# The first expert's tokens: seven tiles gathered early, the eighth put in by a one-hot matmul, and expert blocks 96 wide

## The chip, the cores and the metric

The kernel runs on one core of a Trainium2 chip. The metric is the device time of one execution in microseconds (us). The engines are PE (TensorE: matmuls and transposes), DVE (VectorE), ACT (ScalarE), POOL (GpSimd) and SP (SyncE, which here only issues DMAs). Each engine works through its own instructions in order; semaphores tie the engines together.

## The reference

One layer on 1024 tokens of width 1024: a norm and a wide projection, dilated attention and an RWKV7 branch, an output projection, and then a mixture of experts, which is where the change lies. A router picks one of four groups and two of its eight experts for each token. Cut to what matters:

```python
x = x + mixed @ w_out
h = rms_norm(x, norm2_gain)
grp_prob = softmax(h @ w_group_router + b_group_router); grp_p, grp_idx = top_k(grp_prob, 1)
sel_logits = (h @ w_expert_router + b_expert_router)[group grp_idx]          # 8 of 32
top_p, top_i = top_k(softmax(sel_logits), 2)
gates = grp_p * top_p / sum(top_p); expert_id = grp_idx * 8 + top_i
# for each expert e, over the tokens that chose it (at most two experts a token):
hid = silu(xb @ w_expert_gate[e]) * (xb @ w_expert_up[e])                    # 1024 -> 512
y[token] += gate * (hid @ w_expert_down[e])                                  # 512 -> 1024
x = x + y
```

All of it is float32.

## The kernel before

Products are made at float32 accuracy from two halves: every operand is split into a rounded `hi` and the rest `lo`, and each product is three matmuls (hi x hi, lo x hi, hi x lo).

**The output projection** runs over eight tiles of 128 tokens (the loop `for i in range(8)`), each in two column halves `c`. Behind its matmuls, a tile is added to the residual (`xt`, DVE), multiplied by the norm's gain to `h2` (POOL, or DVE for the last half) and written to HBM (`dH2`, and `out`). `router(i)` transposes `xt` on PE (four transposes for each half), ACT copies them to `hT`, and PE multiplies by the router's weights. `route(i)` is a long chain of small DVE operations: logits `lg`, the two best experts, their one-hots `roh`, a running count over tokens (matmul `pp`), and from it each token's slot within its expert. A one-hot of the slot (`rslot`) times `roh` is summed over all eight tiles in the PSUM tile `pT`: for slot q and expert e it holds the token's index, gate and norm factor. The pieces of `route` are generator steps that `rstep()` interleaves with the next tile's matmuls; behind the last tile they have nothing beside them.

**The experts.** Each of the 32 experts has 96 slots (`CAP`; what goes beyond is done in a branch behind, which this input does not reach). `tbl` is the table of token indices, read from `pT` with 2^20 added, so that an empty slot lies out of bounds. `gather` fetches an expert's rows of `dH2` by an indirect DMA that POOL issues, into one of two `xin` tiles that were zeroed before. `xpose` turns them: eight PE transposes, ACT copies the rounded half (`xTh`), DVE makes the rest (`xTl`). The block is 128 wide there, with 32 rows of zeros. 48 matmuls of 512 columns give gate and up, ACT (Silu) and DVE make `hd` of them, four more transposes give `hTh` and `hTl`, 24 matmuls do the down projection, DVE and ACT scale the result by the gate into `row`, and `add_rows` adds its 96 rows to `out` by an indirect accumulating DMA. Padding rows go to spare rows behind the output (`tba`).

**The weights** of the experts come as 384 chunks of 512 KB, twelve an expert, in the order in which PE wants them: gate and up of expert 0, of expert 1, down of expert 0, gate and up of expert 2, down of expert 1 and so on. Each chunk is split by ACT (`hi`) and DVE (`lo`) into one of nine `u` pairs. The first eight chunks are loaded straight into four of these pairs, so the splits 5 to 8 must wait until the two raw chunks in their pair have been split; from the ninth on, a split waits until PE has used the pair. All later chunks land in a ring of areas (`areas`, 23 of them); a chunk's area is loaded again when its `lo` has been made.

What sets the order: the program is written with a scheduler that orders instructions by priority, except where `manual_schedule` fixes the order as written for some engines. Here DVE, ACT, SP and POOL are fixed from the last tile on until the first expert's transposes are issued.

Of the kernel before, what the change touches and what calls it, by code (L numbers as in the profile page):

```python
# [10 lines left out]
F32 = mybir.dt.float32  # L11
# [35 lines left out]
NPH = 2  # L47
# [5 lines left out]
NL3 = 1  # L53
# [129 lines left out]
def block_kernel(ctx, tc, I, out, dbg=None):  # L183
# [1037 lines left out]
    def route(i, pl, r2):  # L1221
# [106 lines left out]
    p8s = s9.enter_context(tc.tile_pool(name="p8s", bufs=2, reuse_waits="tile"))  # L1328
    s8b = ExitStack()
# [66 lines left out]
    pT = pb([128])  # L1396
# [11 lines left out]
    def split_next(n):  # L1408
        for _ in range(n):
# [6 lines left out]
            hi, lo = pair[:, 0], pair[:, 1]  # L1416
            nc.scalar.activation(hi, raw, AF.Copy)  # L1417
            nc.vector.tensor_tensor(lo, raw, hi.bitcast(F32), op=ALU.subtract)  # L1418
            chunks[key] = (hi, lo)
            cursor[0] += 1  # L1420
            if i >= N0 and i + NR < len(order):
                load_raw(i + NR)

    tailm = ExitStack()
    for i in range(8):
# [3 lines left out]
        h2 = p8.tile([128, S], F32, name="h2", bufs=BH2)  # L1429
# [3 lines left out]
        for c in range(2):  # L1433
# [13 lines left out]
            if i == 7 and c == 1:  # L1447
# [3 lines left out]
                rstep()  # L1451
                tailm.enter_context(tc.manual_schedule(engines={mybir.EngineType.DVE, mybir.EngineType.Activation,
# [36 lines left out]
    xin = [pm.tile([128, D], F32, name=f"xin{i}") for i in range(2)]  # L1489
    row = pm.tile([128, D], F32, name="row")  # L1490
    for t in xin:
        nc.gpsimd.memset(t, 0.0)
# [10 lines left out]
    def gather(dst, src, idx):  # L1503
        dst = dst[0:idx.shape[0]]
        nc.gpsimd.indirect_dma_start(out=dst, out_offset=None, in_=src,  # L1505
                                     in_offset=bass.IndirectOffsetOnAxis(ap=idx, axis=0),
                                     bounds_check=S - 1, oob_is_err=False)
# [27 lines left out]
    gather(xin[0], dH2, tbl[0:CAP, 0:1])  # L1535
# [14 lines left out]
    tailm.close()  # L1550
    tpad = pm.tile([128, 2], F32, name="tpad")
    nc.vector.tensor_scalar(tpad[:, 0:1], tokid[:, 0:1], float(S), None, op0=ALU.add)
    nc.vector.tensor_scalar(tpad[:, 1:2], tpad[:, 0:1], -1.0, float(1 << 20), op0=ALU.mult, op1=ALU.add)
    tba = pm.tile([128, 32], I32, name="tba")
    tocc = pm.tile([128, 32], F32, name="tocc")
    nc.vector.tensor_scalar(tocc, pT[:, 96:128], tpad[:, 1:2], tpad[:, 0:1], op0=ALU.mult, op1=ALU.add)
    nc.vector.tensor_tensor(tba, tocc, pT[:, 0:32], op=ALU.add)
# [5 lines left out]
    for m, e in steps:  # L1563
        if m == 0:
# [4 lines left out]
            for c in range(4):  # L1569
# [133 lines left out]
```

## Time and profile before

| | |
|---|---|
| median of 3 runs | 1723.49 us (1723.04 to 1726.64) |
| the profiled execution | 1724.65 us, its span 1722.9 us |
| PE busy | 96% of the span |
| output projection's last matmul | begins at 1108.27 us |
| first expert's first matmul | begins at 1127.26 us |
| second expert's first matmul | begins at 1143.01 us |
| last matmul | ends at 1710.47 us |

All times are in us from the span's start. Between the projection's last matmul and the first expert's lies a stretch with little on PE; from about 1143 us on PE is never idle until the last two experts.

### The profile page before, as it was taken

To read this page: it belongs to the slowest core of one execution; us is meant where nothing else is said; L and a number is where in the kernel's file an instruction comes from. 1 tells how busy PE (TensorE), PEld (TensorE's weight loads), DVE (VectorE), ACT (ScalarE), POOL (GpSimd) and SP (SyncE) were. 2 spreads that over 40 slices of the span, in tenths; PEclk is the share of its full clock that TensorE was granted. 3 is DMA by queue.
4 is the path that set the end of the run, shared out by engine and by line. 5 is a ranking of instruction groups with operands and counts; after the bars stand their busy time and mean duration, and the time that the engine had idled before them with its cause. 6 is when DMAs were issued, how large, how long until landed. Compare 5 with 4: busy or idle time off the path is not lost. (4 is left out here: it accounts for less than half of the span.)

```text
span 1722.9 us, 25856 instructions
## 1 busy us (share of the span) xinstructions
PE 1646.6 (96%) x9395; PEld 1307.5 (76%) x9396; DVE 1193.8 (69%) x2181; ACT 870.6 (51%) x1315; POOL 290.7 (17%) x314
## 2 busy tenths in 40 slices
PE   8999998999999999999998899889999999999996
PEld 6677777777777777777776677668888888888884
DVE  5638798784553444444335756689999999998985
ACT  4524444423221333344342122378888888887774
POOL 0101103133430000000100221112221222211211
PEclk9999999999999999999998999989999999999998
DMA  8324324466642111111249774679999999999993
GB/s 296 124 85 132 120 86 154 141 239 196 210 140 69 37 44 45 36 41 53 74 146 268 225 288 147 224 255 378 378 375 364 375 375 373 364 370 365 367 370 110
DMA packets 145619, 363.44 MB, mean 211 GB/s; under 512 B 17316, under 2 KB 62772, under 8 KB 145484
## 3 DMA queue, kind: packets, MB, share of 16 engines
q1 hardware_dynamic: 123108, 303.67, 48.9%
q0 software_dynamic: 15872, 50.35, 10.4%
q10 hardware_dynamic: 6504, 7.69, 1.6%
q8 instruction: 76, 1.25, 0.3%
q14 instruction: 59, 0.48, 0.1%
HBM read 307.49 MB, written 62.29 MB: 215 GB/s over the span
## 5 line engine op out<-in xcount | busy, mean ns | idle before, releaser
L1532 PE MATMUL pb<-u,xTh 128*128 128x512 f32 x1024 | 338.6, 406 | 0.5 <-ACT xTh L1527 0.5
L307 PE MATMUL pa<-xlo,wh 128*128 128x512 f32 x736 | 304.9, 414 | 0.0
L307 PE MATMUL pa<-xhi,wh 128*128 128x512 f32 x736 | 300.2, 408 | 2.9 <-DVE qT L905 1.4
L307 PE MATMUL pa<-xhi,wl 128*128 128x512 f32 x736 | 297.9, 405 | 2.3 <-DVE wl L278 2.3
L1418 DVE TENSOR_TENSOR u<-raw,u 128x1024 fp32r<-128x1024 f32 x216 | 254.8, 1221 | 18.6 <-ACT u L1417 15.9
L1417 ACT ACTIVATE u<-raw 128x1024 fp32r<-128x1024 f32 x216 | 223.6, 1056 | 31.6 <-PE pb L1532 18.4
L1532 PEld LDWEIGHTS pb<-u,xTh 128*128 128x128 f32 x1024 | 191.3, 189 | 40.4 <-ACT xTh L1527 1.3
L1532 PE MATMUL pb<-u,xTl 128*128 128x512 f32 x512 | 207.7, 406 | 0.3 <-DVE xTl L1528 0.3
L307 PEld LDWEIGHTS pa<-xlo,wh 128*128 128x128 f32 x736 | 139.9, 190 | 39.1 <-issue 10.3
L307 PEld LDWEIGHTS pa<-xhi,wh 128*128 128x128 f32 x736 | 139.9, 190 | 36.1 <-issue 2.2
L307 PEld LDWEIGHTS pa<-xhi,wl 128*128 128x128 f32 x736 | 139.9, 190 | 33.4 <-DVE wl L278 3.2
L1418 DVE TENSOR_TENSOR u<-mix,u 128x1024 fp32r<-128x1024 f32 x128 | 151.6, 1221 | 11.2 <-ACT u L1417 9.3
L1532 PE MATMUL pa<-u,hTh 128*128 128x512 f32 x512 | 143.4, 401 | 0.9 <-ACT hTh L1527 0.9
L1417 ACT ACTIVATE u<-mix 128x1024 fp32r<-128x1024 f32 x128 | 133.2, 1057 | 16.6 <-PE pb L1532 9.0
L980 DVE SCALAR_TENSOR_TENSOR Sb<-pb,rqk,bias 128x128 f32<-128x128 f32 (+1 forms) x96 | 35.5, 407 | 124.5 <-PE pb L979 116.6
L1511 POOL DMA_INDIRECT out<-row,tba x30 | 78.8, 2627 | 202.1 <-ACT u L1417 171.5
L1532 PEld LDWEIGHTS pb<-u,xTl 128*128 128x128 f32 x512 | 96.9, 189 | 18.5 <-DVE xTl L1528 1.0
L1532 PEld LDWEIGHTS pa<-u,hTh 128*128 128x128 f32 x512 | 93.5, 188 | 22.4 <-ACT hTh L1527 1.5
L276 ACT ACTIVATE wh<-wr 128x1024 fp32r<-128x1024 f32 x49 | 51.8, 1057 | 112.3 <-PE pa L307 106.2
L1532 PE MATMUL pa<-u,hTl 128*128 128x512 f32 x256 | 80.7, 396 | 1.2 <-DVE hTl L1528 1.2
L1505 POOL DMA_INDIRECT xin<-dH,tbl x32 | 38.5, 1204 | 250.3 <-PE pb L1526 247.5
L984 ACT ACTIVATE Sb<-Sb,ML 128x128 f32<-128x128 f32 (+1 forms) x96 | 42.3, 441 | 54.7 <-DVE ML L982 54.7
(415 smaller groups left out, 2829.5 us busy)
## 6 DMA issues: line engine op xcount, KB each, us to landing
raw<-in_w_expert_up SPq DMA_DIRECT2D x72, 512.0 KB, 11.8
raw<-in_w_expert_gate SPq DMA_DIRECT2D x71, 512.0 KB, 5.4
raw<-in_w_expert_down SPq DMA_DIRECT2D x71, 512.0 KB, 11.7
wr<-in_w_in SPq DMA_DIRECT2D x49, 512.0 KB, 3.6
mix<-in_w_expert_down SPq DMA_DIRECT2D x46, 512.0 KB, 13.2
mix<-in_w_expert_gate SPq DMA_DIRECT2D x42, 512.0 KB, 4.9
mix<-in_w_expert_up SPq DMA_DIRECT2D x40, 512.0 KB, 11.9
dGA<-gs POOLq DMA_DIRECT2D x32, 256.0 KB, 2.9
```

The costliest lines, as they stand in the source:

```text
L276: nc.scalar.activation(wh, wr, AF.Copy)
L307: nc.tensor.matmul(ps, a[:, k, :], b[:, k, hs], start=(n == 0), stop=(n == 23))
L980: nc.vector.scalar_tensor_tensor(Sb[:, hh, 0:nk], pS[:, 0:nk], u.rn[:, 0, i, hh:hh + 1], u.bias[:, hh, 256 - nk:], op0=ALU.mult, op1=ALU.add)
L984: nc.scalar.activation(Sb[:, hh, 0:nk], Sb[:, hh, 0:nk], AF.Exp, bias=u.ML[:, i, hh:hh + 1], accum_out=u.ML[:, i, 2 + hh:3 + hh])
L1417: nc.scalar.activation(hi, raw, AF.Copy)
L1418: nc.vector.tensor_tensor(lo, raw, hi.bitcast(F32), op=ALU.subtract)
L1505: nc.gpsimd.indirect_dma_start(out=dst, out_offset=None, in_=src, in_offset=bass.IndirectOffsetOnAxis(ap=idx, axis=0), bounds_check=S - 1, ...
L1511: nc.gpsimd.indirect_dma_start(out=out, out_offset=bass.IndirectOffsetOnAxis(ap=idx, axis=0), in_=src, in_offset=None, compute_op=ALU.add)
L1532: nc.tensor.matmul(ps, x, w, start=first, stop=last)
```

## The change

**The gather.** After tile 6, the table of the first seven tiles is closed (`t6`, and `tb6` for expert 0), and expert 0's rows of tiles 0 to 6 are gathered at once (`xin0`). Tile 7 gets a table of its own (`pTs[1]`), and the two are added for `tbl`. For tile 7's own tokens, `route` makes a one-hot `sel` (token by slot of expert 0), and PE multiplies tile 7's `h7` by it. Both go into one PSUM pair `pt0`: eight transposes of `xin0` start it, eight one-hot matmuls add to it (`turn0`).

**The order.** Three `hi` splits are now ahead of `xTh` of expert 0 on ACT, the others behind it. PE too is written out by hand until expert 0's `hd`, and expert 1's transposes and evacuations come where they are written.

**The width.** Transposes, their evacuations, the stationary operand of all expert matmuls, `hd` and `row` are 96 wide or use 96 rows. `add_rows` uses `tbl`, so empty slots are out of bounds and not written; `tba` and what made it are gone. `NPH` falls from 2 to 0, so there are 21 areas.

```diff
-NPH = 2
+NPH = 0
-NL3 = 1
+NL3 = 3
...
+        if i == 7:
+            ps_ = p8s.tile([128, 2], F32, name="p0", bufs=1)
+            nc.vector.tensor_tensor(ps_[:, 1:2], oh[:, 0, 3, 0:1], oh[:, 1, 3, 0:1], op=ALU.add)
+            nc.vector.tensor_copy(ps_[:, 0:1], pp[:, 0:1])
+            nc.vector.tensor_scalar(sel, rc[:, 72:72 + CAP], ps_[:, 0:1], ps_[:, 1:2], op0=ALU.is_equal, op1=ALU.mult)
...
-            nc.tensor.matmul(pT, slots[s_], oh[:, s_].rearrange("q a e -> q (a e)"), start=(i == 0 and s_ == 0),
-                             stop=(i == 7 and s_ == 1), skip_group_check=True)
+            nc.tensor.matmul(pTs[i // 7], slots[s_], oh[:, s_].rearrange("q a e -> q (a e)"),
+                             start=(i in (0, 7) and s_ == 0), stop=(i in (6, 7) and s_ == 1), skip_group_check=True)
...
+    def turn0(src, by, first):
+        sv = src.rearrange("q (p k) -> q k p", k=8)
+        for k in range(8):
+            nc.tensor.matmul(pt0[k // 4][:, k % 4], sv[:, k], by, start=(first and k % 4 == 0),
+                             stop=(not first and k % 4 == 3), skip_group_check=True)
...
+        if i == 7:
+            pt0 += [pb([4, CAP]) for _ in range(2)]
+            with tc.high_priority(offset=200):
+                turn0(xin0[0:CAP], ident[0:CAP, 0:CAP], True)
         yield from route(i, pl, r2)
...
+                nc.vector.tensor_scalar(t6[:, 0:32], pTs[0][:, 0:32], float(1 << 20), None, op0=ALU.add)
+                nc.vector.tensor_copy(t6[:, 32:96], pTs[0][:, 32:96])
+                nc.vector.tensor_copy(tb6, t6[:, 0:1])
+                nc.gpsimd.memset(xin0, 0.0)
+                gather(xin0, dH2[0:S - 128], tb6[0:CAP], S - 128)
+                pTs[1] = pb([128])
...
+    pem.enter_context(tc.manual_schedule(engines={mybir.EngineType.PE, mybir.EngineType.DVE,
+                                                  mybir.EngineType.Activation, mybir.EngineType.SP,
+                                                  mybir.EngineType.Pool}))
+    turn0(h7, sel, False)
+    split_hi(NL3)
     rstep()
...
-    nc.vector.tensor_scalar(tbl, pT[:, 0:32], float(1 << 20), None, op0=ALU.add)
-    nc.vector.tensor_copy(gr, pT[:, 32:96])
+    split_lo(1)
+    xTn = [pm.tile([128, 8, CAP], F32R, name="xT" + n) for n in "hl"]
+    for q in range(2):
+        nc.scalar.activation(xTn[0][:, 4 * q:4 * q + 4], pt0[q], AF.Copy)
+    for q in range(2):
+        nc.vector.tensor_tensor(xTn[1][:, 4 * q:4 * q + 4], pt0[q], xTn[0][:, 4 * q:4 * q + 4].bitcast(F32),
+                                op=ALU.subtract)
+    split_lo(1)
+    nc.vector.tensor_tensor(tbl, t6[:, 0:32], pTs[1][:, 0:32], op=ALU.add)
+    nc.vector.tensor_tensor(gr, t6[:, 32:96], pTs[1][:, 32:96], op=ALU.add)
...
-                                     in_=src, in_offset=None, compute_op=ALU.add)
+                                     in_=src, in_offset=None, bounds_check=S - 1, oob_is_err=False, compute_op=ALU.add)
...
-            pt = pb([4, 128])
+            pt = pb([4, CAP])
             for j in range(4):
-                nc.tensor.transpose(pt[:, j], sv[:, 4 * q + j], ident)
+                nc.tensor.transpose(pt[:, j], sv[0:CAP, 4 * q + j], ident[0:CAP, 0:CAP])
...
-        nc.tensor.matmul(ps, x, w, start=first, stop=last)
+        nc.tensor.matmul(ps[0:CAP], x, w, start=first, stop=last)
...
                 if e == 0 and c == 3:
-                    xTn = xpose_hi(xin[1], 8, "xT")
+                    xTn = xpose(xin[1], 8, "xT")
...
-            add_rows(rw, tba[0:CAP, e:e + 1])
+            add_rows(rw, tbl[0:CAP, e:e + 1])
```

What this does to the order on the engines is seen at three places. First PE behind the projection's last matmul, before (L1380 transposes tile 7's `xt`, L1392 is the router, L1277 sums the slots, L1526 transposes expert 0's rows):

```order
L1092 MATMUL pa<-woh_7999,mxl 128x512
L1380 MATMUL pb<-ident,xt 128x128 x4
L1392 MATMUL pb<-wr_8584,hT 128x36 x4
L1259 LDWEIGHTS tri
L1259 MATMUL pb<-rA,tri 128x32
L1260 LDWEIGHTS tri
L1260 MATMUL pb<-Acum,tri 128x32
L1277 MATMUL pb<-roh,rslot 128x128 x2
L1538 LDWEIGHTS tri
L1538 MATMUL pb<-Acum,tri 128x32
L1526 MATMUL pb<-ident,xin_9910 128x128 x8
```

And with the change (L1401, L1413 and L1283 are the same three, L1390 is `turn0`, L1588 expert 0's first matmuls):

```order
L1092 MATMUL pa<-woh_7999,mxl 128x512
L1401 MATMUL pb<-ident,xt 128x128
L1390 MATMUL pb<-ident,xin_8576 128x96 x8
L1401 MATMUL pb<-ident,xt 128x128 x3
L1413 MATMUL pb<-wr_8589,hT 128x36 x4
L1259 LDWEIGHTS tri
L1259 MATMUL pb<-rA,tri 128x32
L1260 LDWEIGHTS tri
L1260 MATMUL pb<-Acum,tri 128x32
L1390 MATMUL pb<-sel,h_8575 128x96 x8
L1283 MATMUL pb<-roh,rslot 128x128 x2
```

The eight transposes of the gathered rows have moved from behind the slot sums to a place among tile 7's own transposes, ahead of the router; the one-hot matmuls are new.

Second, ACT from the last routing operation on, before (L1417 is a `hi` split, L1527 `xTh`, L1585 the Silu of `hd`; the first `xTh` pair is expert 0's, the second expert 1's):

```order
L1417 ACTIVATE u<-u 128x1024 x7
L1527 ACTIVATE xTh<-pb 128x512 x2
L1417 ACTIVATE u<-raw_8601 128x1024
L1417 ACTIVATE u<-raw_8603 128x1024
L1417 ACTIVATE u<-raw_8605 128x1024
L1417 ACTIVATE u<-raw_8607 128x1024
L1417 ACTIVATE u<-raw_8609 128x1024
L1417 ACTIVATE u<-raw 128x1024 x2
L1585 ACT_TABLE_LOAD
L1585 ACTIVATE hd<-pb,gr 128x512
L1527 ACTIVATE xTh<-pb 128x512 x2
```

And with the change (L1443 is the `hi` split, L1555 and L1583 are `xTh`):

```order
L1443 ACTIVATE u<-u 128x1024 x3
L1555 ACTIVATE xTh<-pb 128x384 x2
L1328 DMA mxh<-in_w_expert_up 128x1024
L1330 DMA mxh<-in_w_expert_down 128x1024
L1443 ACTIVATE u<-u 128x1024 x5
L1443 ACTIVATE u<-raw_8606 128x1024
L1443 ACTIVATE u<-raw_8608 128x1024
L1443 ACTIVATE u<-raw_8610 128x1024
L1443 ACTIVATE u<-raw_8612 128x1024
L1443 ACTIVATE u<-raw_8614 128x1024
L1443 ACTIVATE u<-raw 128x1024 x3
L1583 ACTIVATE xTh<-pb 128x384 x2
```

Expert 0's `xTh` comes after three splits where it came after eight. Expert 1's comes after sixteen, as against fifteen splits, the table load and `hd` before.

Third, PE at the turn from expert 0 to expert 1 with the change (before, the eight transposes stood singly among expert 0's last twenty matmuls):

```order
L1588 MATMUL pb<-u,xTh 96x512 x2
L1588 MATMUL pb<-u,xTl 96x512
L1582 MATMUL pb<-ident,xin_9936 128x96 x8
L1588 MATMUL pb<-u,xTh 96x512 x4
L1588 MATMUL pb<-u,xTl 96x512
```

Expert 1's transposes have moved behind all of expert 0's matmuls, and four of expert 1's matmuls stand ahead of its first one that needs `xTl`.

## Rows read from the trace of the kernel before

**Rows 1.** Busy time, share of the span and instructions of PE (the page).

```profile
PE 1646.6 (96%) x9395; PEld 1307.5 (76%) x9396; DVE 1193.8 (69%) x2181; ACT 870.6 (51%) x1315; POOL 290.7 (17%) x314
```

**Rows 2.** Timeline of PE: start, duration, operation; in brackets the idle time before.

```profile
1109.45 0.66 PE L1380 MATMUL pb<-ident,xt 128*128 128x128 f32 x4 [0.78 <-DVE xt L1463]
...
1116.67 1.36 PE L1277 MATMUL pb<-roh,rslot 128*128 128x128 f32 x4 [1.24 <-DVE roh L1276]
...
1125.43 1.94 PE L1526 MATMUL pb<-ident,xin 128*128 128x128 f32 x8 [6.69 <-DMA xin<-dH,tbl]
1127.26 1.22 PE L1532 MATMUL pb<-u,xTh 128*128 128x512 f32 x2
```

**Rows 3.** Timeline of DVE in the same stretch.

```profile
1112.36 0.22 DVE L1226 SCALAR_TENSOR_TENSOR lg<-pb,r,br 128x4 f32<-128x4 f32 x1
...
1118.07 0.19 DVE L1498 TENSOR_SCALAR tbl<-pb 128x32 int32<-128x32 f32 x1 [0.89 <-PE pb L1277]
...
1118.46 1.22 DVE L1418 TENSOR_TENSOR u<-u 128x1024 fp32r<-128x1024 f32 x1
...
1119.86 6.90 DVE L1418 TENSOR_TENSOR u<-u 128x1024 fp32r<-128x1024 f32 x6
```

**Rows 4.** Timeline of ACT in the same stretch, up to the second expert's start.

```profile
1114.69 1.04 ACT L1417 ACTIVATE u<-u 128x1024 fp32r<-128x1024 f32 x1
...
1116.51 3.90 ACT L1417 ACTIVATE u<-u 128x1024 fp32r<-128x1024 f32 x4 [0.78 <-issue]
1121.12 1.06 ACT L1417 ACTIVATE u<-u 128x1024 fp32r<-128x1024 f32 x1 [0.71 <-DVE u L1418]
...
1142.37 1.08 ACT L1527 ACTIVATE xTh<-pb 128x512 fp32r<-128x512 f32 x2
```

**Rows 5.** Timeline of POOL from tile 7's first half on.

```profile
1102.46 1.28 POOL L1467 TENSOR_TENSOR h<-xt,g 128x512 f32<-128x512 f32 x1 [5.74 <-DVE xt L1463]
...
1119.14 1.47 POOL L1505 DMA_INDIRECT xin<-dH,tbl  x1 [2.49 <-issue]
```

**Rows 6.** DMA issues, 1095 to 1150: median us from issue to landing.

```profile
xin<-dH,tbl POOLq DMA_INDIRECT x4, 5.7
```

**Rows 7.** The gathers of 1150 to 1200, by tile: issue to landing.

```profile
DMA to landing us min/median/max: 7.7/7.8/8.2
```

**Rows 8.** Timeline of PE: the second expert's first matmuls.

```profile
1143.01 0.97 PE L1532 MATMUL pb<-u,xTh 128*128 128x512 f32 x3 [0.54 <-ACT xTh L1527]
```

**Rows 9.** Busy time by stretch: length, engines, granted clock (PEclk), DMA share, GB/s.

```profile
903.20:907.80 4.60, 0.01 (x1) 0.00 (x0) 2.21 (x4) 0.63 (x1) 0.00 (x0) 0.99 0.99 364
907.80:911.20 3.40, 3.37 (x7) 2.26 (x8) 2.24 (x7) 1.32 (x3) 0.54 (x1) 0.52 0.88 272
...
1130.00:1135.00 5.00, 5.00 (x17) 3.94 (x17) 2.66 (x3) 2.44 (x3) 0.00 (x0) 0.70 0.59 155
```

**Rows 10.** Timeline of PE over one expert of the steady part.

```profile
1161.12 0.62 PE L1532 MATMUL pb<-u,xTh 128*128 128x512 f32 x2
...
1171.45 0.27 PE L1526 MATMUL pb<-ident,xin 128*128 128x128 f32 x1
...
1171.79 0.27 PE L1526 MATMUL pb<-ident,xin 128*128 128x128 f32 x1
...
1179.11 0.62 PE L1532 MATMUL pb<-u,xTh 128*128 128x512 f32 x2
```

**Rows 11.** PE's weight loads by line: ns min/median/max; stationary shape (rows*columns) last.

```profile
L1022 PEld LDWEIGHTS pb<-ident,ML x48: 81/85/85, 638.0 to 891.8; 128*4 128x4 f32 x48
L1005 PEld LDWEIGHTS pb<-PT,Vt x280: 132/136/137, 571.4 to 890.9; 128*64 128x64 f32 x140
L1526 PEld LDWEIGHTS pb<-ident,xin x232: 185/189/191, 1171.2 to 1676.7; 128*128 128x128 f32 x116
```

**Rows 12.** DMA queues from 1160 to 1690: packets, MB, share of 16 engines.

```profile
q1 hardware_dynamic: 48573, 176.85, 86.4%
q0 software_dynamic: 6468, 18.91, 16.1%
```

More of the change, by code (lines that the diff above doesn't have):

```diff
@@ L1328, in block_kernel @@
     p8s = s9.enter_context(tc.tile_pool(name="p8s", bufs=2, reuse_waits="tile"))
+    h7 = p8s.tile([128, S], F32, name="h7", bufs=1)
+    xin0 = p8s.tile([128, S], F32, name="xin0", bufs=1)
+    sel = p8s.tile([128, CAP], F32, name="sel", bufs=1)
+    t6 = p8s.tile([128, 96], F32, name="t6", bufs=1)
+    tb6 = p8s.tile([128, 1], I32, name="tb6", bufs=1)
     s8b = ExitStack()
@@ L1406, in block_kernel, with split_hi @@
     cursor = [0]
-    def split_next(n):
+    his = []
+    def split_hi(n):
         for _ in range(n):
@@ L1415, in split_next, with split_lo, gather @@
             pair = ph.tile([128, 2, 1024], F32R, name="u", bufs=NU)
-            hi, lo = pair[:, 0], pair[:, 1]
-            nc.scalar.activation(hi, raw, AF.Copy)
+            nc.scalar.activation(pair[:, 0], raw, AF.Copy)
+            his.append((i, key, raw, pair[:, 0], pair[:, 1]))
+            cursor[0] += 1
+    def split_lo(n):
+        for _ in range(min(n, len(his))):
+            i, key, raw, hi, lo = his.pop(0)
             nc.vector.tensor_tensor(lo, raw, hi.bitcast(F32), op=ALU.subtract)
             chunks[key] = (hi, lo)
-            cursor[0] += 1
             if i >= N0 and i + NR < len(order):
                 load_raw(i + NR)
+    def split_next(n):
+        for _ in range(n):
+            split_hi(1)
+            split_lo(1)
+    def gather(dst, src, idx, rows=S):
+        dst = dst[0:idx.shape[0]]
+        nc.gpsimd.indirect_dma_start(out=dst, out_offset=None, in_=src,
+                                     in_offset=bass.IndirectOffsetOnAxis(ap=idx, axis=0),
+                                     bounds_check=rows - 1, oob_is_err=False)
     tailm = ExitStack()
@@ L1428, in block_kernel @@
         ss2 = p8s.tile([128, 2], F32, name="ss2")
-        h2 = p8.tile([128, S], F32, name="h2", bufs=BH2)
+        h2 = h7 if i == 7 else p8.tile([128, S], F32, name="h2", bufs=BH2)
         mh, ml = nxt
@@ L1488, in block_kernel @@
     pm = s9.enter_context(tc.tile_pool(name="pm", bufs=1, reuse_waits="tile"))
-    xin = [pm.tile([128, D], F32, name=f"xin{i}") for i in range(2)]
+    xin = [xin0, pm.tile([128, D], F32, name="xin1")]
     row = pm.tile([128, D], F32, name="row")
-    for t in xin:
-        nc.gpsimd.memset(t, 0.0)
+    nc.gpsimd.memset(xin[1], 0.0)
+    pem = ExitStack()
+    pem.enter_context(tc.manual_schedule(engines={mybir.EngineType.PE, mybir.EngineType.DVE,
[3 more added lines that the diff above has]
+    split_hi(NL3)
     rstep()
@@ L1497, in block_kernel @@
     tbl = cst.tile([128, 32], I32, name="tbl")
-    nc.vector.tensor_scalar(tbl, pT[:, 0:32], float(1 << 20), None, op0=ALU.add)
-    nc.vector.tensor_copy(gr, pT[:, 32:96])
-    rstep()
[L1503 to L1507, printed above, removed]
+    split_lo(1)
[5 more added lines that the diff above has]
+                                op=ALU.subtract)
+    split_lo(1)
+    nc.vector.tensor_tensor(tbl, t6[:, 0:32], pTs[1][:, 0:32], op=ALU.add)
+    nc.vector.tensor_tensor(gr, t6[:, 32:96], pTs[1][:, 32:96], op=ALU.add)
+    rstep()
     def add_rows(src, idx):
@@ L1531, in acc @@
     def acc(ps, w, x, first, last):
-        nc.tensor.matmul(ps, x, w, start=first, stop=last)
+        nc.tensor.matmul(ps[0:CAP], x, w, start=first, stop=last)
     hid = {}
-    gather(xin[0], dH2, tbl[0:CAP, 0:1])
     gather(xin[1], dH2, tbl[0:CAP, 1:2])
@@ L1538, in block_kernel @@
     nc.tensor.matmul(pcn, tri[:, 128:256], Acum, start=True, stop=True)
-    for _ in range(NL3):
-        split_next(1)
     while todo:
         load_raw(todo.pop(0), nc.scalar)
+    split_lo(NL3)
     split_next(LEAD - cursor[0])
-    xTn = xpose(xin[0], 8, "xT")
     cmax = cst.tile([128, 1], F32, name="cmax")
@@ L1549, in block_kernel @@
     nc.vector.tensor_copy(cnt[:, 1:33], pcn[0:1])
[L1550 to L1557, printed above, removed]
     def xpose_hi(src, kt, name):
@@ L1582, in block_kernel @@
                 if e == 0 and c == 3:
-                    xTn = xpose_hi(xin[1], 8, "xT")
+                    xTn = xpose(xin[1], 8, "xT")
             hd = pm.tile([128, 512], F32, name="hd", bufs=2)
-            nc.scalar.activation(hd, pg_, AF.Silu, scale=rsl[:, e:e + 1])
-            nc.vector.scalar_tensor_tensor(hd, pu_, rsl[:, e:e + 1], hd, op0=ALU.mult, op1=ALU.mult)
+            hc, rc_ = hd[0:CAP], rsl[0:CAP, e:e + 1]
+            nc.scalar.activation(hc, pg_[0:CAP], AF.Silu, scale=rc_)
+            nc.vector.scalar_tensor_tensor(hc, pu_[0:CAP], rc_, hc, op0=ALU.mult, op1=ALU.mult)
             hid[e] = hd
+            if e == 0:
+                pem.close()
+                tailm.close()
             if e == N_EXP - 1:
@@ L1605, in block_kernel @@
             rw = row if e < N_EXP - 2 else xin[e % 2]
-            nc.vector.tensor_scalar(rw[:, 0:512], pd[0], gat[:, e:e + 1], None, op0=ALU.mult)
-            nc.scalar.activation(rw[:, 512:1024], pd[1], AF.Copy, scale=gat[:, e:e + 1])
-            add_rows(rw, tba[0:CAP, e:e + 1])
+            gc = gat[0:CAP, e:e + 1]
+            nc.vector.tensor_scalar(rw[0:CAP, 0:512], pd[0][0:CAP], gc, None, op0=ALU.mult)
+            nc.scalar.activation(rw[0:CAP, 512:1024], pd[1][0:CAP], AF.Copy, scale=gc)
+            add_rows(rw, tbl[0:CAP, e:e + 1])
     s9.close()
```

8 lines of the change are left out of this document (5 added, 3 removed).

## The prediction, made before the changed kernel ran

> **What bounds the kernel now.** I read the page's engine table first: PE is busy for 96% of the span [rows 1], so time can only come from shorter PE work or from the few stretches in which PE waits. PE's timeline shows the longest of these just where the change is made. After the last tile's transposes PE does little until the gathered rows of expert 0 land: 6.69 us of idle time at a stretch, and expert 0's first matmul begins at 1127.26 [rows 2]. The DVE timeline says what is serial in it: logits at 1112.36, the index table at 1118.07 [rows 3], then the gather on POOL at 1119.14 [rows 5], eight transposes at 1125.43 [rows 2]. From expert 1's start at 1143.01 [rows 8] PE runs without a gap: one expert takes 1161.12 to 1179.11, 17.99 us, for 72 matmuls and 12 transposes. From one single transpose to the next, with one matmul between, are 0.34 us [rows 10]. With matmul M and transpose T, 72M + 12T = 17.99 and M + T = 0.34 give M = 0.232 and T = 0.108 us.
>
> So there are two places to cost: the start of the experts, where chains count, and 31 experts behind it, where only PE's own nanoseconds count.
>
> **The start: when does expert 0 begin?** The early gather can be issued once POOL has done `h` of tile 7's first half, at 1102.46 + 1.28 = 1103.74 [rows 5]. Gathers land 5.7 us after issue around here [rows 6], 7.8 us when the queues are full [rows 7]: at 1109.5 to 1111.8, if issued at about 1103.8 to 1104. PE wants it at about 1109.6, after one of tile 7's transposes, and the order shows three transposes and the router queued behind it. At 1109.5 it costs the eight transposes themselves, 8 x 0.108 = 0.9 us; of these some 0.5 are hidden, since the logits wait for the norm's chain on DVE until shortly before 1112.36 anyway. That is 0.35 us. At 1111.8 the three transposes end at about 1113.1, the copy to `hT` and four router matmuls at about 1114.3, and the logits come 2.0 us late. I take **+1.0** for this delay, between the ends (0.35 to 2.0).
>
> Then the routing runs as before, with three more small DVE operations (0.57 us by their neighbours) ahead of `sel`. The eight one-hot matmuls start at about 1116.2; eight transposes at the same half clock took 1.94 us [rows 2], so the first four are done at about 1117.2. ACT's three splits start at 1114.69 and go at 3.90 / 4 = 0.975 us each [rows 4], to 1117.7. `xTh` follows, 0.47 us for 384 columns (1.08 for two of 512 [rows 4]). Expert 0 starts at about 1118.3 instead of 1127.26: 9 us earlier, before the delay.
>
> **What that is worth is decided at expert 1.** ACT has the splits 8 to 15 ahead of expert 1's `xTh`. Split 8 waits for `lo` 7, as split 5 waits for `lo` 1 now [rows 4]. DVE is free for `lo` at about 1117.8 (now 1118.46, behind four operations of 0.6 together that move back, and behind the three new ones). Up to `lo` 7 it does eight `lo` of 1.18 us (1.15 to 1.22 [rows 3]), two `xTl` of 0.55 and some 1.1 us of small work: 1129.4. Eight splits of 0.975 bring ACT to 1137.2, and `xTh` to 1137.7. PE is long done: 48 matmuls of 0.232 from 1118.3, the first part at half clock (now half clock lasts until three fifths into 1130 to 1135, by the mean of 0.70 [rows 9], 7.6 us after the transposes start at 1125.43), end at about 1133.3, eight transposes at 1134.2. So the old wait goes and a **new one of 3 to 4 us** comes in front of expert 1. DVE makes seven `lo` from 1130.5 to 1138.8 ahead of `xTl`, which is ready at 1139.35; PE has four matmuls to do until it needs that (0.93 us) and waits 0.75 again. Expert 1's start moves from 1143.01 [rows 8] to 1137.7, less that wait: **-4.55**.
>
> **The clock.** With PE idle from 903.2 to 907.8 the next 3.4 us ran at a granted clock of 0.52 [rows 9], the lower of the two levels (1.2 GHz): a loss of 1.7 us. The new wait is nearly as long. I take **+1.7** (0 if the clock stays up, 3.4 if the drop lasts twice as long).
>
> **96 columns: transposes.** The cost is bounded by what a shorter stream and a shorter weight load can give. Loads take 85 ns for 4 columns, 136 for 64, 189 for 128 [rows 11], so 0.83 ns a column: 27 ns less for 96. A transpose still loads 128 columns, and its identity streams 96 instead of 128, a quarter of 0.108 us or 27 ns less. In a run of transposes each next load still has 128 columns and binds, so only the last of a run is shorter, where a 96-column load follows. The changed order has 215 runs of transposes behind the start, hence **-5.8** (215 x 27 ns). Bounds: nothing, if the stream isn't what binds, and 12 x 31 x 27 ns = 10.0.
>
> The Trainium skill ("TensorE: Matmul & The Clock Gate", LDWEIGHTS) has a load scale with its columns and not its rows; the three load rows agree, with the same slope. The same page's "Weight-path perf modes" speaks against the change: a fast weight load is on only for 128 weights that aren't FP32, so 96 columns would lose it. The rows show no such load, since 128 columns lie on the line through 4 and 64. By that rule the transposes' -5.8 would fall away, since the load behind them would be no shorter, and the sum would be -3.85; by the rows it is -9.65.
>
> **96 columns: matmuls.** All 2304 of 512 columns keep their stream. No row has such a matmul with fewer stationary columns. If every nanosecond of the shorter load came through, it would be 27 ns x 2304 = 62 us; but loads run beside matmuls (PE 96%, PEld 76% of the span [rows 1]), and one of 0.189 fits into an M of 0.232. So I let at most a sixth through, 4 ns or 9 us, and nothing as the other end, and stay near nothing, at about 1 ns: **-2**.
>
> **Costed at nothing.** Evacuations of 384 columns shorten ACT and DVE, which PE doesn't wait for in the steady part. `sel`, `t6` and the second table lie beside matmuls of tile 7 or are counted above. Expert 1's gather needs `tbl`, ready at about 1121.7, plus 7.8 us: 1129.5, ahead of its transposes. Two fewer areas and the dropped padding go together: loads got 176.85 MB in 530 us [rows 12], so twelve chunks take 18.85 us against PE's 17.99, and PE lives on the stock ahead of it (21 areas are 33 us of load time). Now that gap eats 30 x 0.86 = 26 us. If the dropped padding (about a third of the rows added) gives back some 0.5 us an expert, as its share of the 16.1% of the software queue suggests [rows 12], the stock lasts with PE 0.25 us faster.
>
> **Sum**: -4.55 + 1.0 + 1.7 - 5.8 - 2 = -9.65. The profiled execution took 1724.65 (span 1722.9, 1.75 around it), the median is 1723.49, 1.16 lower; taken from the median the forecast is 1714. By the measurement's spread, 0.2% (3.4 us) is about what can be told from no change: faster is below 1720.0, slower above 1726.9.
>
> **Rivals** (times from the median).
> *The start's gain is eaten and 96 wide gives nothing on PE.* The gather lands at 1111.8 (+2.0), the clock drops (+1.7), transposes stay bound by their 128-column loads: -4.55 + 3.7 = -0.85, **1722.6**. For it: M and T are near what loads could set; against: the load after a transpose has 96 columns. By the Trainium skill's rule on the fast load ("Weight-path perf modes", above) it would come out here too.
> *All of it counts.* Matmuls lose 4 ns each (-9), the clock stays up, the gather is in time: -4.55 + 0.35 - 5.8 - 9 = -19, **1704.5**. Against: the load fits beside the stream.
> *The weights' DMA becomes the bound.* If dropping the padding saves no DMA time, 30 x (0.86 + 0.25) = 33 us of gap meet 33 us of stock, of which the earlier start has used 4.5: about +5, **1719**. For it: DVE's next reload can't come before `lo` 8, at 1131 as now.
> *Slower: a matmul with 96 stationary columns takes longer.* With no gain on the matmuls the sum is -7.65; it decides from 11.1 us, 4.8 ns on each of 2304. At 7 ns it is +16, **1732**. For it only that no row shows the form; against, the load rows, where fewer columns never cost more.
>
> **How the numbers follow.** Forecast (5 to 16 us faster) 0.56; nothing from the width 0.17; all counts 0.12; DMA 0.08; slower 0.07. The range reaches from between the forecast and the all-counts case to the no-gain case: 1704 to 1722; the forecast's own range is 1708 to 1719. Faster takes the forecast, all-counts and most of the DMA case, with a little of the second rival: 0.77. Same: 0.15. Slower: 0.08.
>
> **What the changed profile would show.** The eight transposes of `xin0` (L1390) between tile 7's, with no more than 2 us of wait on the gather; logits 0.35 to 2 us after 1112.36; expert 0's first matmul near 1119.3, with the delay; a wait of 3 to 4 us on `xTh` (L1583) before expert 1, then half clock for about 3.4 us; expert 1 near 1138.7; an expert in 17.7 us; single transposes 27 ns cheaper; ACT's `hi` never waiting for a DMA long enough to stop PE. I am wrong if the gather lands after 1112, if expert 1 doesn't wait, if an expert still takes 17.98 us, or if PE waits on weights near the end.

## The result, and the profile after

The changed kernel takes 1737.27 us (median of 12 runs, 1730.35 to 1744.49) against 1724.36 for the kernel before on the same chip (12 runs): a ratio of 1.0063, 95% interval [1.0046, 1.008]. It is **slower by 0.63%, some 10.8 us** (the two medians lie 12.9 apart), where 10 us less were forecast. The profiled execution took 1739.06 (span 1737.1).

Up to the change both programs do the same, but the stretches at half clock fall differently there from one execution to the next, so the output projection's last matmul starts at anything from 1102.0 to 1121.6 in the fourteen profiles of this study. All times below are therefore counted from that matmul, called **P**. It is in the kernel before (timeline of PE)

```profile
1108.27 0.40 PE L1092 MATMUL pa<-woh,mxl 128*128 128x512 f32 x1
```

and from P to the end of the span the kernel before needs 1722.9 - 1108.27 = 614.6 us, the changed one 1737.1 - 1112.91 = 624.2. These **9.6 us** are what has to be found.

The changed kernel's timeline of PE, from P to expert 0's first matmuls (it answers to [rows 2]):

```profile
1112.91 0.40 PE L1092 MATMUL pa<-woh,mxl 128*128 128x512 f32 x1
1114.09 0.33 PE L1401 MATMUL pb<-ident,xt 128*128 128x128 f32 x1 [0.79 <-DVE xt L1512]
1116.72 4.10 PE L1390 MATMUL pb<-ident,xin 96*128 96x96 f32 x16 [2.30 <-DMA xin<-dH,tb]
1120.61 0.84 PE L1401 MATMUL pb<-ident,xt 128*128 128x128 f32 x3
1122.14 1.92 PE L1413 MATMUL pb<-wr,hT 128*128 128x36 f32 x8 [0.69 <-ACT hT L1402]
1126.96 0.21 PE L1259 MATMUL pb<-rA,tri 128*128 128x32 bf16 x1 [2.89 <-DVE rA L1257]
1127.01 0.19 PE L1260 MATMUL pb<-Acum,tri 128*128 128x32 bf16 x1
1128.01 4.12 PE L1390 MATMUL pb<-sel,h 128*128 128x96 f32 x16 [0.81 <-DVE rscr L1276]
1131.92 1.11 PE L1283 MATMUL pb<-roh,rslot 128*128 128x128 f32 x4
1134.74 0.21 PE L1593 MATMUL pb<-Acum,tri 128*128 128x32 bf16 x1 [1.71 <-DVE Acum L1286]
1134.79 1.15 PE L1588 MATMUL pb<-u,xTh 128*96 128x512 f32 x2
```

The gather of `xin0` landed 2.30 us too late for PE, which waits for it with three of tile 7's transposes and the router queued behind. The eight turns then count x16 and last 3.9 us, as do the eight one-hot matmuls. Expert 0 starts at P + 21.9 instead of P + 19.0.

On DVE and ACT (timelines; they answer to [rows 3] and [rows 4]) the delay reads like this:

```profile
1124.10 0.22 DVE L1226 SCALAR_TENSOR_TENSOR lg<-pb,r,br 128x4 f32<-128x4 f32 x1 [7.15 <-PE pb L1413]
...
1132.68 0.56 DVE L1557 TENSOR_TENSOR xTl<-pb,xTh 128x384 fp32r<-128x384 f32 x1 [1.30 <-ACT xTh L1555]
...
1134.52 0.17 DVE L1286 TENSOR_TENSOR Acum<-Acum,rA 128x32 bf16<-128x32 bf16 x1
...
1141.87 8.02 DVE L1450 TENSOR_TENSOR u<-raw,u 128x1024 fp32r<-128x1024 f32 x7
```

```profile
1126.43 2.94 ACT L1443 ACTIVATE u<-u 128x1024 fp32r<-128x1024 f32 x3
```

The logits come at P + 11.2 (before: 1112.36 - 1108.27 = P + 4.1 [rows 3]), and the 7.1 us stay: expert 0's first split on ACT starts at P + 13.5, before at P + 6.4 [rows 4]. On DVE the update of `Acum` stands behind `xTl`, and PE's count matmul (L1593), ahead of all of expert 0, waits 1.71 us for it. The last row is the first `lo` whose raw chunk lies in an area that a load will fill again; its first one ends at 1143.1.

SP, which issues the weights' loads, shows what hangs on that `lo` (timelines, the changed kernel, then the one before):

```profile
1115.67 0.84 SPq L1328 DMA_DIRECT2D mix<-in_w_expert_gate  x1
1143.10 2.60 SPq L1330 DMA_DIRECT2D raw<-in_w_expert_down  x3
...
1690.69 4.09 SPq L1330 DMA_DIRECT2D mix<-in_w_expert_down  x4
```

```profile
1111.60 0.33 SPq L1322 DMA_DIRECT2D mix<-in_w_expert_gate  x1
1130.84 0.34 SPq L1324 DMA_DIRECT2D raw<-in_w_expert_down  x1
...
1678.65 4.13 SPq L1324 DMA_DIRECT2D raw<-in_w_expert_down  x4
```

SP's loads begin again at P + 30.2 instead of P + 22.6, **7.6 us later**. From there to the last load's issue (its start, 0.3 us ahead of the end of the last row) it is 551.4 us in the one and 551.6 in the other, and from that to the end 42.6 and 40.4. The three differences, +7.6 - 0.3 + 2.2, are the 9.6 but for rounding. Busy time by stretch of the changed kernel says the same of the DMA (columns as in [rows 9]):

```profile
1117.00:1121.00 4.00, 4.00 (x18) 4.00 (x19) 0.00 (x0) 0.00 (x0) 0.18 (x1) 0.52 0.89 342
1121.00:1125.00 4.00, 2.38 (x11) 1.83 (x9) 0.86 (x7) 0.68 (x2) 0.00 (x0) 0.50 0.01 3
1125.00:1130.00 5.00, 2.23 (x10) 2.16 (x11) 4.75 (x29) 3.54 (x7) 0.00 (x0) 0.50 0.00 0
```

Nothing moves from 1121 to 1130: all areas are full but two, whose loads ACT issues behind `xTh`, at 1132.17 and 1132.55, and these, with two gathers, are what moves before SP begins again. Over the 50 us from P + 2, and the 518 us behind them, the same view shows for the kernel before and for the changed one

```profile
1110.30:1160.30 50.00, 36.90 (x160) 29.70 (x161) 43.22 (x87) 35.45 (x43) 7.14 (x7) 0.80 0.80 266
1160.30:1678.30 518.00, 518.00 (x2424) 432.67 (x2423) 482.49 (x484) 428.38 (x485) 109.72 (x56) 1.00 1.03 370
```

```profile
1114.90:1164.90 50.00, 40.21 (x169) 31.08 (x170) 37.57 (x81) 31.21 (x39) 5.92 (x5) 0.76 0.61 216
1164.90:1682.90 518.00, 516.46 (x2403) 371.81 (x2402) 469.29 (x483) 407.14 (x481) 110.20 (x57) 1.00 1.01 363
```

The second column from the end is the DMA share: 0.80 is 10 us without work, 0.61 is 19.5. In the 518 us the DMA is full in both. PE reads 516.46 of 518 there, almost full too, and that is deceptive: one expert in the middle (timeline of PE, answering to [rows 10]) takes 17.85 us, but from expert 21 to expert 30 `hd` on DVE comes every 18.77:

```profile
1205.60 0.62 PE L1588 MATMUL pb<-u,xTh 128*96 128x512 f32 x2
...
1215.97 0.25 PE L1582 MATMUL pb<-ident,xin 96*128 96x96 f32 x1
...
1216.29 0.25 PE L1582 MATMUL pb<-ident,xin 96*128 96x96 f32 x1
...
1223.45 0.62 PE L1588 MATMUL pb<-u,xTh 128*96 128x512 f32 x2
```

```profile
1633.94 0.75 DVE L1632 SCALAR_TENSOR_TENSOR hd<-pb,gr,hd 96x512 f32<-96x512 f32 x1 [2.02 <-PE pb L1588]
...
1652.70 0.75 DVE L1632 SCALAR_TENSOR_TENSOR hd<-pb,gr,hd 96x512 f32<-96x512 f32 x1 [2.01 <-PE pb L1588]
```

PE's timeline says where the 9.6 us arise. Expert 2 and expert 23 of the changed kernel begin with the rows

```profile
1169.88 0.62 PE L1588 MATMUL pb<-u,xTh 128*96 128x512 f32 x2
...
1545.05 0.40 PE L1588 MATMUL pb<-u,xTh 128*96 128x512 f32 x1
```

and expert 23 of the kernel before with

```profile
1538.70 0.62 PE L1532 MATMUL pb<-u,xTh 128*128 128x512 f32 x2
```

From P, expert 2 is 4.1 us late (57.0 against 52.85 [rows 10]). Up to expert 23 that shrinks to 1.7 (432.1 against 430.4), since an expert takes 0.13 us less. The other 7.9 us are lost behind expert 23, where seven experts start 18.77 apart.

A matmul's row lasts 0.39 us where the next starts 0.23 behind it, so a wait shorter than the difference leaves no idle time on PE. It shows on the weight loads (the table of waits from 1560 to 1690: us in total, times, longest):

```profile
PEld pa L1588 <- DVE u L1450: 8.9, 21, 0.7
```

The queues from 1160 to 1690, which answer to [rows 12]:

```profile
q1 hardware_dynamic: 48575, 176.87, 88.6%
q0 software_dynamic: 6384, 14.85, 12.0%
```

A chunk is 0.524 MB, so q1 needs 530 x 0.524 / 176.87 = 1.57 us for one, 18.8 for an expert's twelve, and that is the pace of the last experts. q1 moved the same 176.9 MB before, when the scatter's padding still went through q0 (18.91 MB then).

### The profile page after: what moved, and what is told of

Same layout as the page of the kernel before. It is cut to its first block, busy times and chain, and to the rows that moved or that the text cites. A ratio compares the mean times of both kernels' runs of the same rounds, so it can differ in the third digit from the quotient of the medians.

```text
span 1737.1 us, 25932 instructions
## 1 busy us (share of the span) xinstructions
PE 1664.9 (96%) x9419; PEld 1256.7 (72%) x9420; DVE 1181.8 (68%) x2183; ACT 851.7 (49%) x1315; POOL 289.1 (17%) x314
## 5 line engine op out<-in xcount | busy, mean ns | idle before, releaser
L1588 PE MATMUL pb<-u,xTh 128*96 128x512 f32 x1024 | 342.0, 405 | 1.9 <-ACT hd L1631 1.7
L1450 DVE TENSOR_TENSOR u<-raw,u 128x1024 fp32r<-128x1024 f32 x198 | 233.8, 1216 | 14.1 <-ACT u L1443 11.1
L1588 PEld LDWEIGHTS pb<-u,xTh 128*96 128x96 f32 x1024 | 166.2, 164 | 69.3 <-DVE u L1450 4.1
L1443 ACT ACTIVATE u<-raw 128x1024 fp32r<-128x1024 f32 x198 | 201.5, 1053 | 19.9 <-PE pb L1588 11.9
L1588 PE MATMUL pb<-u,xTl 128*96 128x512 f32 x512 | 205.6, 402 | 0.0
L1443 ACT ACTIVATE u<-mix 128x1024 fp32r<-128x1024 f32 x144 | 146.9, 1053 | 14.3 <-PE pb L1588 8.0
L1588 PE MATMUL pa<-u,hTh 128*96 128x512 f32 x512 | 147.5, 402 | 2.3 <-DVE u L1450 1.5
L1588 PEld LDWEIGHTS pa<-u,hTh 128*96 128x96 f32 x512 | 79.9, 164 | 42.2 <-DVE u L1450 11.7
L1567 POOL DMA_INDIRECT out<-row,tbl x30 | 70.5, 2350 | 221.1 <-ACT row L1657 152.6
L1588 PEld LDWEIGHTS pb<-u,xTl 128*96 128x96 f32 x512 | 83.3, 163 | 29.3
L1588 PE MATMUL pa<-u,hTl 128*96 128x512 f32 x256 | 80.5, 396 | 0.7 <-DVE hTl L1584 0.7
```

Of the source, the lines that this page charges most:

```text
L1443: nc.scalar.activation(pair[:, 0], raw, AF.Copy)
L1588: nc.tensor.matmul(ps[0:CAP], x, w, start=first, stop=last)
```

## The experiments

Two theories of the late experts could be held. **Loads:** they begin 7.6 us later into two areas fewer, PE uses up the stock sooner and then goes at their pace. **Order:** the compiled order on ACT and DVE puts fewer splits ahead of `hd` near the end, and `hd` waits for PE, so the splits stand behind it although the data has landed; for this spoke that no ACT split there waits for a DMA. Each ratio is against the kernel before on the same chip, with its 95% interval; idle DMA is 50 us x (1 - share) of the 50 us from P + 2.

| kernel | ratio | expert 0 | idle DMA | last load issued | end |
|---|---|---|---|---|---|
| before | 1 | P + 19.0 | 10.0 | P + 574.2 | P + 614.6 |
| changed | 1.0063 | 21.9 | 19.5 | 581.5 | 624.2 |
| hold_lead | 1.005 [1.0027, 1.0073] | 23.0 | 19.5 | 581.5 | 625.5 |
| changed_fewer_loads | 0.9985 [0.9971, 0.9999] | 21.7 | 18.5 | 557.0 | 613.9 |
| before_fewer_loads | 0.9995 [0.9975, 1.0014] | 19.4 | 10.0 | 552.1 | 613.0 |
| width_alone | 1.0003 [0.9983, 1.0022] | 19.0 | 9.0 | 574.8 | 615.1 |
| gather_alone | 1.0028 [1.001, 1.0046] | 21.7 | 18.5 | 580.8 | 619.5 |
| turn_behind_router | 1.0018 [0.9999, 1.0037] | 15.3 | 12.5 | 573.9 | 618.1 |
| before_21_areas | 1.0022 [1.0007, 1.0036] | 21.0 | 14.0 | 578.4 | 617.9 |
| changed_24_areas | 1.0045 [1.0023, 1.0067] | 22.0 | 15.0 | 578.9 | 619.7 |
| width_and_early_splits | 1.0023 [1.0003, 1.0044] | 22.0 | 12.0 | 575.3 | 616.8 |
| width_25_areas | 1.0006 [0.9985, 1.0028] | 21.5 | 9.0 | 572.3 | 616.8 |
| behind_pcn_24_areas | 0.999 [0.9971, 1.0008] | 13.6 | 7.5 | 570.8 | 614.1 |
| behind_pcn_24_areas_held | 0.9991 [0.9973, 1.0008] | 13.4 | 8.0 | 568.7 | 610.8 |

**hold_lead** keeps DVE, ACT and SP in program order, so that the splits keep their distance ahead of `hd`.

```diff
                 tailm.close()
+                tailm.enter_context(tc.manual_schedule(engines={mybir.EngineType.DVE, mybir.EngineType.Activation, mybir.EngineType.SP}))
```

> The changed kernel, with DVE, ACT and SP kept in written order through all experts, so that seven splits stand ahead of every hd (in the changed kernel this falls from 8 to 1 between experts 15 and 21 and stays at 1). Theory 'order': the last ten experts lose 0.93 us each because the lo of the down chunks stand behind hd on DVE; here all experts take about 17.85 us and the time falls by 8 us, to 2 or 3 us above the kernel before. Rival 'DMA': the loads themselves need 18.8 us an expert and 21 areas hold too little; then the wait only moves to ACT, which waits for landings, the last ten experts still take 18.7 us and the time stays about 11 us above the kernel before.

The time is that of the changed kernel, and the wait appears where the loads' theory wants it, on ACT in the last third (its timeline):

```profile
1625.78 1.06 ACT L1443 ACTIVATE u<-raw 128x1024 fp32r<-128x1024 f32 x1 [2.25 <-DMA raw<-in_w_expert_up]
```

So the order theory falls in this form: with seven splits ahead, ACT waits for the DMA 51 times from 1478 on, 27 us in all, and nothing is won. That the compiled order costs nothing is not shown. A trace records the landing of one load in eight; from the 265th chunk to the 360th such a chunk lies landed for 7.6 us on the mean in the changed kernel until ACT splits it, and for 0.1 in hold_lead, where PE in turn waits up to 2.83 us for an `xTh` that stands on ACT behind splits. An order between the two was not tried.

**changed_fewer_loads, before_fewer_loads** leave out every eighth load from the 41st chunk on; the split takes the chunk before it again, so one eighth of the weights used there are others, with the same instructions on every compute engine.

```diff
+    def gone(i):
+        return i >= 40 and i % 8 == 7
...
-            raw = raws.pop(key)
+            raw = last[0] if gone(i) else raws.pop(key)
+            last[0] = raw
```

> The changed kernel with the same loads left out (every eighth chunk from the 41st on is split from the chunk before it, so the output is of other weights there). Theory 'loads': the changed kernel ends late because the first reload of an area comes about 8 us later after the projection and two areas fewer hold 3 us less, and 353 loads of 1.57 us then set the end; without that bound only PE counts: 4 us lost at the start, 0.12 us an expert gained, so within 2 us of the other kernel with fewer loads, and some 10 us faster than the changed kernel. Rival 'PE': what the start lost and what PE does per expert set the end; then it stays 6 or more us slower than the other.

> The kernel before, in which from the 41st weight chunk on every eighth is not loaded: its split reads the chunk before it again, so PE, ACT and DVE do the same work and the output is of other weights there. Weight loads then need 16.5 us an expert instead of 18.8. Both theories: before, PE bounds nearly all the way, so experts take 17.98 us to the end and the time falls by 0 to 3 us.

With 43 loads fewer the changed kernel loses its whole surplus, and its `hd` come 17.41 and 18.36 us apart by turns, 17.88 on the mean, to the end. The kernel before gains nothing measurable. So fewer loads undo the loss, and the kernel before was not yet bound by its loads; before_21_areas below shows how near to it it was. The compiled order changes with the loads, though: the splits keep their distance ahead of `hd` to the end here. This pair of runs can't part the two theories, only hold_lead does.

**width_alone** is the kernel before with 96-wide blocks and the padding dropped; **gather_alone** is the changed kernel with 128-wide blocks for the experts 1 to 31 (the padding still dropped).

```diff
-                nc.tensor.transpose(pt[:, j], sv[0:CAP, 4 * q + j], ident[0:CAP, 0:CAP])
+                nc.tensor.transpose(pt[:, j], sv[:, 4 * q + j], ident)
```

> The kernel before, with 96 wide expert blocks and padding rows dropped, but the old gather, order of the start and 23 areas. Theory 'order': an expert takes 17.85 instead of 17.98 us, but with the shorter blocks the scheduler lets the splits ahead of hd run out from the 19th expert on (in the kernel before from the 24th, at 1 only for the last two), so some seven experts take 18.8 us: in all 2 to 4 us slower than before. Rival 'width harmless': all experts take 17.85 us, 3 to 4 us faster than before.

> The changed kernel with blocks of experts 1 to 31 128 wide again (expert 0 stays 96 wide; padding rows still dropped, 21 areas). Theory: the start is about 4 us later than before at expert 2, as in the changed kernel, experts take 17.98 us until the splits ahead run out at the 26th, and five or six lose up to 0.9 us each: 7 to 9 us slower than before. Rival 'the width did it all': the time comes back to that of the kernel before or 3 us below.

The width alone gives nothing, which neither expectation had: its experts take 17.87 us and expert 2 starts 1.9 us earlier (P + 50.9 against 52.85), but experts 26 to 29 take 18.75, and the end is the same. The loss comes with the early gather. Its size alone, 0.28%, is below the changed kernel's 0.63%, though the last load is issued at almost the same time; what follows that load is 38.8 us here and 42.6 there. The stretch runs from 38.8 to 44.5 us in the kernels with all loads, and the traces show what varies in it. The third load from the end, the last whose landing is recorded, lands at 1702.04 in the changed kernel. ACT splits that chunk 12.2 us later, behind a `hd` that waits for PE (ACT's timeline):

```profile
1713.64 0.69 ACT L1631 ACTIVATE hd<-pb,gr 96x512 f32<-96x512 f32 x1 [2.62 <-PE pb L1588]
1714.22 1.99 ACT L1443 ACTIVATE u<-mix 128x1024 fp32r<-128x1024 f32 x2
```

In gather_alone it is 8.3 us. From the split to the end it is 22.9 us in both. Over the ten kernels with all loads and a compiled order, the first time varies from 8.3 to 13.7 us and the second from 21.6 to 23.2. So what varies is how long landed data lies behind the compiled order; why it comes out so differently stays open.

**turn_behind_router** puts the eight turns of `xin0` behind the last tile's router on PE.

```diff
+            if i == 7:
+                pe7.enter_context(tc.manual_schedule(engines={mybir.EngineType.PE}))
             for k in range(4 if i == 7 else 0, 8):
                 nc.tensor.matmul(pl, hT[:, k], wr36[:, k], start=(k == 0), stop=(k == 7))
```

> The changed kernel, with the eight turns of the gathered rows behind tile 7's router on PE instead of among its transposes. Theory 'turn ahead of the router': the logits came 7.1 us later after the projection's last matmul than before (wait for the gather 2.3, sixteen passes at half clock 3.9), and all behind them; here the logits come back to about 4.1 us after that matmul, expert 0 begins some 6 us earlier than in the changed kernel, and the time falls by about 6, to 5 us above the kernel before. Rival 'experts' own chains': ACT and DVE with sixteen splits ahead of expert 1 set the start anyway; then the time falls by less than 2 us.

PE's timeline shows no wait for the gather any more, and the turns beside work of DVE:

```profile
1110.20 1.08 PE L1416 MATMUL pb<-wr,hT 128*128 128x36 f32 x8 [0.69 <-ACT hT L1402]
1111.31 4.09 PE L1390 MATMUL pb<-ident,xin 96*128 96x96 f32 x16
```

Expert 0 starts 6.6 us earlier than in the changed kernel, SP's loads begin again at P + 23.6 instead of 30.2, the last is issued 7.6 earlier, and the ratio falls from 1.0063 to 1.0018, by some 7.8 us. The place of the eight turns is most of the loss.

**before_21_areas** takes two areas from the kernel before (`NPH = 2` to `0`, as in the change); **changed_24_areas** gives the changed kernel three more, opened where expert 0 begins.

```diff
-    areas = ["mr2"] * NRAW2 + ["mr"] * NRAW + list(range(8)) + ["mx"] * 2 + ["ph"] * NPH
+    areas = ["mr2"] * NRAW2 + ["mr"] * NRAW + list(range(8)) + ["mx"] * 2 + ["ph"] * NPH + ["px"] * 3
```

> The kernel before with two areas fewer for weight chunks (21 instead of 23), nothing else. Theory 'loads': the stock is two chunks or 3.1 us smaller, and since the loads were just in time before, the time rises by 2 to 3 us. Rival 'areas are free': PE never waited for a chunk before the last two experts, so the time stays the same within 1 us.

> The changed kernel with three more areas for weight chunks (24 instead of 21), in space that is free once the tile loop's tiles are gone. Theory 'loads': the end is set by the loads, and three chunks more in stock at the start are 3 x 1.57 = 4.7 us: from 10.8 to about 6 us above the kernel before. Rival 'start': what was lost ahead of expert 2 sets the end; no change.

Two areas cost the kernel before 0.22% (3.3 us from P to the end), but not by the stock alone: the order at the start changes too, and PE waits there for an `xTh` that stands on ACT behind the splits (PE's timeline).

```profile
1131.84 1.65 PE L1532 MATMUL pb<-u,xTh 128*128 128x512 f32 x3 [3.68 <-ACT xTh L1527]
```

Of these 3.25 us, 0.64 are there from expert 1 to expert 28, and the other 2.6 come behind it. Three areas gave the changed kernel 4.5 us (0.18% by the ratios), and its experts slow down only from expert 25 on. In these profiles an area is thus worth 1.3 to 1.5 us, near the 1.57 that its load takes.

**Two misses.** width_and_early_splits splits two chunks ahead of the last tile's residual, to let loads begin earlier; width_25_areas gives width_alone two more areas.

> The kernel before with 96 wide blocks and padding dropped (as in the run with the width alone, which took as long as before), and the splits of the first two chunks moved ahead of the last tile's residual, into 5 us in which DVE waits for PE. Theory 'loads': the first reload comes two lo, 2.4 us, earlier, and with it the end: 2 to 3 us faster than before. Rival 'PE or its order': the experts start no earlier, so the time stays that of the width alone, within 1 us of before.

> The kernel before with 96 wide blocks and padding dropped, and 25 areas instead of 23. Theory 'loads': the width alone brought nothing because the loads took over as the bound; two more chunks in stock let 3 us of PE's gain through, to 2 to 3 us below the kernel before. Rival 'width brings nothing to PE over the whole': same as before within 1 us.

Neither tested what it was made for. ACT's early splits had to wait for PE's matmuls of the projection (P is 1107.47 there), and the residual waited behind them on DVE; the two extra loads went out just ahead of expert 0's gather, whose landing took 8.7 us (5.2 in width_alone), and PE waited 9.21 us for it (before: 6.69 [rows 2]). The rows of ACT and DVE, then the row of PE:

```profile
1107.67 2.00 ACT L1417 ACTIVATE u<-u 128x1024 fp32r<-128x1024 f32 x2 [3.47 <-PE pa L1092]
...
1108.76 2.36 DVE L1418 TENSOR_TENSOR u<-u 128x1024 fp32r<-128x1024 f32 x2 [6.23 <-ACT u L1417]
```

```profile
1133.48 1.52 PE L1530 MATMUL pb<-ident,xin 96*128 96x96 f32 x8 [9.21 <-DMA xin<-dH,tbl]
```

**behind_pcn_24_areas** joins the turns behind the router, the three areas, and the step that updates `Acum` ahead of the first `lo` (the count matmul `L1593`, which stands ahead of expert 0 on PE, waited 1.71 us for it); the last kernel adds hold_lead's order.

```diff
+    rstep()
     split_lo(1)
...
-    rstep()
```

> The changed kernel with the turns of the gathered rows behind the router, the update of Acum ahead of the first xTl on DVE (so that the count's matmul no longer holds PE for 1.7 us in front of expert 0), and 24 areas. Theory 'loads': 3 us above before with the turns moved, less 1 to 2 for the earlier chain on DVE, less 4.7 for the areas: 2 to 4 us below the kernel before. Rival 'PE': then the earlier start of expert 0 counts as a whole, 8 us below it.

> The same, and DVE, ACT and SP in written order through all experts, seven splits ahead. Theory 'loads': the order is not what binds, so within 2 us of the same kernel without it. Rival 'order': the last experts no longer wait for their lo, 5 us or more faster than without it.

Expert 0 now starts 5.4 to 5.6 us earlier than before the change and the DMA idles 2.0 to 2.5 us less. The time is 0.1% below the kernel before, inside what can't be told from no change: the loss is undone, and nothing is won.

## Why the prediction was wrong

Two steps failed, and they work through one another.

- **The delay by the early turns, "+1.0" (0.35 to 2.0).** The gather was issued at 1108.49, P - 4.4, as I had it (1103.8, against P at 1108.27). Its landing took 8.1 us, a little over the range's upper end, and PE waited 2.30; the range held that nearly. What failed is the price of the turns. They were put at 8 x 0.108, a transpose at full clock, but the clock had fallen to half when they ran (0.52 from 1117 to 1121, behind the wait), and they are fp32 matmuls and not transposes: sixteen records of 0.243 us, 3.9 us. The logits came 7.1 us late: 2.3 + 3.9, and 1.3 for three transposes and the router's eight, now at half clock, less the 0.45 that stayed hidden behind the norm's chain. That such a matmul counts twice could be read in [rows 2], where the two slot matmuls of L1277 count x4. The one-hot turns were sized wrong likewise (4.12 for 1.94). The Trainium skill ("FP8 and Floating Point Precision", TensorE Precision Notes) has four passes for a true fp32 matmul; here each left two records, each as long as a transpose of 128 columns at half clock (1.94 / 8 = 0.243 [rows 2]), so the time is twice a transpose's.
- **The loads, "costed at nothing".** I counted 33 us of stock against 26 of deficit and let the stock last. By the same sum it had to fail once loads begin 7.6 us later: 33 - 7.6 = 25 us against 30 x (18.85 - 17.85) = 30. The sum was too generous besides: before_21_areas has 33 us against 26 as well, and lost 2.6 us at its end. In the changed kernel PE ran dry from expert 23 on and lost 7.9 us there. I had tied the first reload to expert 0's `lo` in a rival ("The weights' DMA becomes the bound", 0.08) and not carried the delay over to it. Its mechanism is what happened, its 1719 was not: it still credited an earlier start.
- **The dropped padding gives loads nothing.** The rows left q0 (18.91 to 14.85 MB), and q1 stayed at 176.9 MB in 530 us. The 0.5 us an expert that I hoped for are not there.
- **Expert 0 and expert 1.** Expert 0 was to start 9 us earlier, less the delay; it started 2.9 later. The wait of 3 to 4 us for `xTh` in front of expert 1 did not come. In its place PE waits 1.74 us behind expert 1's first two matmuls, for ACT's `hd` of expert 0 behind the table load (PE's timeline):

```profile
1150.89 0.81 PE L1588 MATMUL pb<-u,xTh 128*96 128x512 f32 x2 [1.74 <-ACT hd L1631]
```

Half clock for 3.4 us followed (granted clock 0.66 from 1150 to 1155), so the "+1.7" came out right, though behind another wait. Expert 1, which began 0.8 us late, takes 21.4 us instead of 18.1, and so expert 2 is 4.1 late.
- **The width, "-5.8" and "-2".** The forecast was 0.25 us an expert. Measured are 17.98 - 17.85 = 0.13: M + T is now 1216.29 - 1215.97 = 0.32, and 72M + 12T = 17.85 gives T = 0.087 and M = 0.233, so transposes lost some 20 ns and the matmuls nothing (the rows' hundredths leave T open by 8 ns or so). The shorter load did come, some 163 ns for an expert's matmul where it was 188, and gave the matmuls nothing. The 0.13 is not credited in any case, since the loads' 18.8 us per expert set the end (width_alone).
- The rival of slower matmuls with 96 columns did not happen: M is 0.233 for 0.232.

## What to carry to other kernels

Where a stream runs at its own limit behind a stock of buffers, ask first what an edit does to the moment at which the stream can start again and to the number of buffers; nanoseconds saved on the engine that looks 96% busy only empty the stock sooner. Work that is moved forward on an in-order engine is priced with everything queued behind it, here three transposes and the router on which the routing and all splits hang. And a matmul is priced by a row of the same kind and type, with its count of records, not by a transpose that has the same shape.

## What the runs showed of the hardware

- An fp32 matmul by a 0/1 matrix left two records, together 0.49 us at half clock; a transpose leaves one of 0.243. The router's eight records at the same clock, with 36 streamed columns instead of 96, lasted 0.24 each as well (1.92 / 8), and PE's weight loads were busy for 4.00 of the 4.00 us from 1117 to 1121. So the streamed columns did not set this time; that the loads did was not tested.
- The loads' pace did not depend on what the software queue carried beside them: 1.57 us for 512 KB with 18.91 and with 14.85 MB of other traffic, while the total fell from 370 to 363 GB/s.
- 128-wide experts took 17.86 us in gather_alone and 17.98 in the kernel before, with the same matmuls and transposes. There the same two equations (0.34 between single transposes, 1204.84 and 1205.18 on PE's timeline) give T = 0.110 and M = 0.230. The mean of some 1000 steps from one matmul to the next agrees: 0.2347 us before, 0.2324 in gather_alone and 0.2342 in the changed kernel. Which part of the changed layout gives matmuls 2 ns was not tried.
